# Gate products of a linear recurrence: one fp32 product, or three one-pass products of split operands, in a decoder layer on one Trainium2 core

## The chip, the cores and the metric

The kernel runs on one core of a Trainium2 chip, as one program. The metric is the device time of one execution in microseconds (us). Engines are named as in the profile: PE is TensorE (matrix products), PEld its weight loads, DVE VectorE, ACT ScalarE, POOL GpSimd, SP the queue that issues most transfers from memory.

## The reference, cut to what matters

One layer of a hybrid decoder is computed for 256 prompt tokens and 8 sample tokens (264 columns in all, `N`), with a model width of 2048, everything in float32. The first half of the layer is one combined projection of the normalised input, whose columns feed two groups: a gated linear recurrence (RG-LRU) and an mLSTM.

```
xn = rmsnorm(x);  z = xn @ w_in
xr, conv_new = causal_conv(z[rgx], conv_buf, conv_w, conv_b)      # 4 taps along the tokens
r  = sigmoid(block_diag(xr, w_rg_a, b_rg_a))                      # 8 blocks of 128 x 128
ig = sigmoid(block_diag(xr, w_rg_x, b_rg_x))
h  = rglru(xr, r, ig, lam, h0)                                    # scan over the tokens
y_rg = rmsnorm(h * gelu(z[rgg]))
h_ml = mlstm(q, k, v, logi, logf, C0, n0, m0)                     # q, k, v, gates also from z
y_ml = rmsnorm(h_ml, per head) * sigmoid(z[o])
x = x + concat(y_rg, y_ml) @ w_out
x = x + cross_attention(rmsnorm(x), memory);  x = x + swiglu(rmsnorm(x));  y = rmsnorm(x)
```

The two `block_diag` products are the gates of the title: for each of eight blocks of 128 channels, two products of a 128x128 weight with the block's 264 convolved tokens.

## The kernel before, in words

Tokens lie along the free axis, channels on the 128 partitions. All large products are built from one helper, `mm3`: both operands are split into a high part, rounded to the one-pass fp32r form, and a low part, the rest, and three one-pass products are added up (high by high, high by low, low by high). Weights arrive from memory by SP into `raw` tiles of 128x1024 and are split there: ACT copies the high half into a `W` tile (four buffers), DVE subtracts it from `raw` to make the low half. This is done per half step, one step ahead of PE (`LS`), and the loads run three steps ahead (`LD`).

The main loop goes over `steps`. A step of the projection is one tile of 128 output columns: 16 chunks by three products, 48 matmuls of 128x264 in a bank of PSUM (`mm`). Steps 0 to 7 give the convolution's inputs (rgx), step 8 the mLSTM's exponent gates, 9 to 16 q and k, 17 to 24 v, 25 to 32 rgg, 33 to 40 the output gate o, then w_out and the rest. The result of a step is evacuated by DVE and ACT one step later (`pend`); the evacuations of steps 4, 5 and 34 to 36 are held back, and the latter are run at the end of step 36:

```
if i not in (4, 5, 34, 35, 36):
    ... for e, x in pend: e(x)
ps = pef(i)
if i == 36:
    ... for e, x in pend: e(x)
```

All other work is written as generators ("side work") that are advanced after each step as far as the engines' clocks of a price table allow (`pump`; a `yield` gives the work back to the loop, `yield STEP` to the next step). Small products of PE that belong to side work are inserted into the steps' matmuls by `later(..., after=k)`: not before k more groups of three products have been issued. `finish(cond)` issues all such products that are outstanding at once. From this program order a scheduler builds the queue of each engine; the queues of SP are issued as written.

What the change and the prediction touch: `evac_rgx(n)` scales a block of rgx by `rstd` (the first norm) into a tile `z`; `rg_conv(n)` runs the four taps on DVE with a temporary `t` and leaves `xr`; `rg_gen` loads the gate weights (`wrg`, two transfers), runs the convolution and the two gate products of each block, and then the recurrence. The products stand in banks of tag `ax`. `ml_norm` is the norm at the end of the mLSTM: `sums` adds up squares on PE, from which DVE makes the small tiles `r`, `v`, `f` (128x12, `c` in the profile); `turn` transposes `f` by three products with the identity, ACT and DVE split the result into `hl` (4x264), and `scale(h)` spreads it over the partitions by two products a head:

```
later(lambda h=h: sums(h), after=1)
later(turn, after=19)
later(lambda h=h: scale(h), after=1 if h else 6)
```

`evac_o(0)`, the evacuation of the first o step, needs the normed heads: it calls `finish(lambda: ml.get("nn", 0) > j // 2)`. Tiles of tag `B` (128x1088) have 26 buffers, `t` six; every engine instruction is recorded under line 63, that of the wrapper which adds up prices, so that the profile is read by tile names.

Of the kernel before, what the change touches and what calls it, by code (L numbers as in the profile page):

```python
# [10 lines left out]
F32 = mybir.dt.float32  # L11
F32R = mybir.dt.float32r
I32 = mybir.dt.int32
AF = mybir.ActivationFunctionType
# [3 lines left out]
P = 128  # L18
# [4 lines left out]
N = T + NS  # L23
# [21 lines left out]
STEP = object()  # L45
# [45 lines left out]
def layer_kernel(ctx: ExitStack, tc, xT, memT, vec, wrg, w_in, w_out, w_q, w_k, w_v, w_o,  # L91
# [3 lines left out]
    act, dve, pe = Engine(nc.scalar, price_act), Engine(nc.vector, price_dve), Engine(nc.tensor, price_pe)  # L95
# [10 lines left out]
    def nm(s):  # L106
        uid[0] += 1
        return f"{s}_{uid[0]}"

    def view(t, shape, skip=0):  # L110
        v = t[:, skip: skip + int(np.prod(shape[1:]))]
        if len(shape) == 2:
            return v
        names = "abcd"[:len(shape) - 1]
        return v.rearrange(f"p ({' '.join(names)}) -> p {' '.join(names)}",
                           **{c: int(n) for c, n in zip(names[1:], shape[2:])})

    def B(shape, dt=F32, skip=0):
        return view(sb.tile([P, SLOT], dt, tag="B", bufs=NB, name=nm("B")), shape, skip)
# [109 lines left out]
    def mm3(ps, a, b, start, stop):  # L229
        ah, al = a  # L230
        bh, bl = b
        pe.matmul(ps, ah, bh, start=start, stop=False)
        pe.matmul(ps, ah, bl, start=False, stop=False)
        return pe.matmul(ps, al, bh, start=False, stop=stop)
# [65 lines left out]
    def bank(tag="mm"):  # L300
        return psm.tile([P, 512], F32, tag=tag, bufs=4, name=nm(tag))
# [26 lines left out]
    def V(name, j=0, w=1):  # L328
        o = _V[name][0] + j
        return vecs[:, o: o + w]  # L330
# [119 lines left out]
    rg = {"zn": 0}  # L450
# [39 lines left out]
    def evac_rgx(n):  # L490
        def f(ps):
            if "xr" not in rg:
                rg["xr"] = Arr(RGB)
            z = B([P, 2, 292])
            zi = z[:, 0, :]
            dve.memset(zi[:, 0:3], 0.0)
            smp = zi[:, 259:291].rearrange("p (b j) -> p b j", j=4)
            hist = V("cst", n * 24, 24).rearrange("p (b j) -> p b j", j=3)
            act.activation(smp[:, :, 0:3], hist, AF.Copy)
            dve.tensor_mul(zi[:, 3:259], ps[:, :T], rstd[:, :T])  # L500
            dve.tensor_mul(smp[:, :, 3:4], ps[:, T:N].rearrange("p (b j) -> p b j", j=1),
                           rstd[:, T:N].rearrange("p (b j) -> p b j", j=1))
            rg["z", n] = z
            if n >= 4:
                rg["zn"] = n + 1
        return f

    def rg_conv(n):
        z = rg.pop(("z", n))
        zi, t = z[:, 0, :], z[:, 1, :]  # L510
        smp = zi[:, 259:291].rearrange("p (b j) -> p b j", j=4)
        act.activation(cpo[:, n, :], zi[:, 256:259], AF.Copy)
        act.activation(cso[:, n, :, :], smp[:, :, 1:4], AF.Copy)
        w = [V("cw", j * 8 + n) for j in range(4)]
        dve.tensor_scalar(t[:, :288], zi[:, 0:288], w[0], V("cb", n), op0=OP.mult, op1=OP.add)
        dve.scalar_tensor_tensor(t[:, :288], zi[:, 1:289], w[1], t[:, :288], op0=OP.mult, op1=OP.add)
        dve.scalar_tensor_tensor(t[:, :288], zi[:, 2:290], w[2], t[:, :288], op0=OP.mult, op1=OP.add)
        xr = rg["xr"](n)
        dve.scalar_tensor_tensor(xr[:, :T], zi[:, 3:259], w[3], t[:, :T], op0=OP.mult, op1=OP.add)
        ts = t[:, 259:291].rearrange("p (b j) -> p b j", j=4)  # L520
        dve.scalar_tensor_tensor(xr[:, T:N].rearrange("p (b j) -> p b j", j=1), smp[:, :, 3:4], w[3],
                                 ts[:, :, 0:1], op0=OP.mult, op1=OP.add)

    def rg_gen():
        wr = [B([P, 8, P]), B([P, 8, P])]
        for j in range(2):
            sp.dma_start(wr[j], wrg[:, j * 8: j * 8 + 8, :])
        r, ig = Arr(RGB), Arr(RGB)
        for n in range(RGB):
            while rg["zn"] <= n:  # L530
                yield STEP
            rg_conv(n)
            yield STEP
            for t, j, b in ((r, 0, "ba"), (ig, 1, "bx")):
                ps = bank("ax")
                pe.matmul(ps[:, :N], wr[j][:, n, :], rg["xr"](n), start=True, stop=True)
                last = act.activation(t(n), ps[:, :N], AF.Sigmoid, bias=V(b, n))
            yield 0.1
        yield STEP
        xr, c = rg["xr"], rg["c"]  # L540
        e2 = Arr(RGB)

        for q in range(2):
            for n in range(4 * q, 4 * q + 4):
                with tc.issue_after(last.ins):
                    act.activation(e2(n), r(n), AF.Exp, scale=c[:, 8 + n: 9 + n])
                    le = act.activation(r(n), r(n), AF.Exp, scale=c[:, n: n + 1])
            dve.tensor_scalar(e2.tile(q), e2.tile(q), 1.0, -1.0, op0=OP.min, op1=OP.add)
            dve.tensor_mul(ig.tile(q), ig.tile(q), xr.tile(q))
            yield 2.0  # L550
        rg["le"] = le
        while "emc" not in ml:
            yield STEP
        for q in range(2):
            with tc.issue_after(ml["emc"].ins):
                act.activation(e2.tile(q), e2.tile(q), AF.Sqrt, scale=-1.0)
            dve.tensor_mul(ig.tile(q), ig.tile(q), e2.tile(q))
            yield 1.2
        h = Arr(RGB)
        rg["h"] = h  # L560
        for n in range(RGB):
            dve.tensor_tensor_scan(h(n)[:, :T], r(n)[:, :T], ig(n)[:, :T], 0.0, op0=OP.mult, op1=OP.add)
            yield 0.6
        h0 = V("h0", 0, 64).rearrange("p (n b) -> p n b", b=NS)
        for q in range(2):
            hq, rq_, iq = (t.tile(q)[:, :, T:N] for t in (h, r, ig))
            dve.tensor_mul(hq, rq_, h0[:, 4 * q: 4 * q + 4, :])
            dve.tensor_add(hq, hq, iq)
            act.activation(hlast[:, 4 * q: 4 * q + 4, :], h.tile(q)[:, :, T - 1: N], AF.Copy)
        pool_e.dma_start(o_h, hlast)  # L570
        pool_e.dma_start(o_cp, cpo)
        pool_e.dma_start(o_cs, cso)
        yield 0.3
# [882 lines left out]
    for i, (src, cols, pef, evf, need) in enumerate(steps):  # L1456
        load_piece(i + LD - 1)
        if i == 5:
            st["rg"] = side(rg_gen(), 0)
# [17 lines left out]
        ps = pef(i)  # L1477
# [141 lines left out]
```

## Time and the profile before

| | before |
|---|---|
| runs | 1540.1, 1539.87, 1538.17 us |
| median | 1539.87 us |
| the profiled execution: its own time | 1535.74 us |
| its span (first to last instruction) | 1534.0 us |
| mean granted clock of TensorE | 0.998 |
| busy: PE, DVE, ACT, POOL | 1524.8, 1059.3, 784.0, 126.1 us |
| share of the span: PE, DVE, ACT, POOL | 99%, 69%, 51%, 8% |
| PE's matmuls | 12028 |

The profile is of a single execution; its time is 4.1 us under the median of the runs. Busy times are sums over all instructions of an engine. Idle time before an instruction is put down to what released it. In the rows of groups a form such as `128*128 128x264` is the weight tile and the moving tile; "x48" is the number of instructions in a row. Positions in the text are microseconds from the start of the span.

### The profile page before, as it was taken

The page shows a single profiled execution, that of the slowest core. Times are in us where ns is not written, and L with a number is a line of the kernel's source. Part 1 is how long each engine was busy: PE and PEld are TensorE (multiplying, and loading weights), DVE is VectorE, ACT ScalarE, POOL GpSimd, SP SyncE. Part 2 cuts the span into 40 slices and gives each one's busy share as a digit, 9 for nine tenths or more (in the row PEclk, how much of TensorE's full clock was granted, in tenths as well). Part 3 has the DMA queues.
Part 4 walks back from the last instruction along what each step waited for, and adds up shares of the span by engine and source line. Part 5 has one row for each costly group of instructions (what it writes and reads, how often), then busy time and mean ns, then how long its engine had stood idle before and what let it go on. Part 6 is the DMA issues. An engine that isn't in the chain of part 4 may idle for free.

```text
span 1534.0 us, 29990 instructions
## 1 busy us (share of the span) xinstructions
PE 1524.8 (99%) x12028; PEld 1490.9 (97%) x12028; DVE 1059.3 (69%) x2013; ACT 784.0 (51%) x1234; POOL 126.1 (8%) x189
## 2 busy tenths in 40 slices
PE   9999999999999999999999999999999999999998
PEld 9999999999998888899999999999999999999997
DVE  7976988778898989966665555545555545555554
ACT  7555875655556666654444444334444433344463
POOL 0001210000223434400000000000000000000000
PEclk9999999999999999999999999999999999999999
DMA  8646996556798788755555555555555555555563
GB/s 300 203 154 203 322 327 207 194 179 233 266 341 326 246 339 332 248 160 188 188 180 182 190 179 184 188 179 184 188 179 185 187 180 186 185 180 186 158 225 121
DMA packets 94043, 329.17 MB, mean 215 GB/s; under 512 B 10992, under 2 KB 12448, under 8 KB 93904
## 3 DMA queue, kind: packets, MB, share of 16 engines
q1 hardware_dynamic: 78768, 274.62, 53.2%
q0 software_dynamic: 14992, 52.63, 9.7%
q8 instruction: 94, 1.54, 0.4%
q14 instruction: 45, 0.37, 0.1%
q10 hardware_dynamic: 144, 0.01, 0.0%
HBM read 314.36 MB, written 12.86 MB: 213 GB/s over the span
## 4 chain that ended last, share of the span: by engine, by line
PE 99%; DVE 0%; DMA 0%; ACT 0%; DVEq 0%; issue 0%; ACTq 0%
PE mm L63 94%; PE ax L63 5%; DVE B L63 0%; DMA raw<-w_in 0%; ACT W L63 0%; ACT B L63 0%; DVEq L1596 0%; ACTq L63 0%
## 5 line engine op out<-in xcount | busy, mean ns | idle before, releaser
L63 PE MATMUL mm<-B,W 128*128 128x264 f32 (+2 forms) x11008 | 1363.0, 285 | 0.0
L63 PEld LDWEIGHTS mm<-B,W 128*128 128x128 f32 x11008 | 1340.5, 188 | 11.7
L63 ACT ACTIVATE W<-raw 128x1024 fp32r<-128x1024 f32 (+2 forms) x520 | 536.7, 1034 | 640.3 <-PE mm L63 434.2
L63 DVE TENSOR_TENSOR W<-raw,W 128x1024 fp32r<-128x1024 f32 (+2 forms) x520 | 619.4, 1193 | 347.4 <-ACT W L63 346.0
L63 PE MATMUL mm<-W,B 128*128 128x512 f32 x384 | 92.4, 395 | 0.0
L63 PEld LDWEIGHTS mm<-W,B 128*128 128x128 f32 x384 | 70.9, 188 | 16.1
L63 DVE TENSOR_TENSOR t<-mm,rstd 128x264 f32<-128x264 f32 x104 | 44.7, 431 | 44.2 <-PE mm L63 44.1
L1511 POOL TENSOR_TENSOR B<-B,rstd 128x264 f32<-128x264 f32 x4 | 2.8, 738 | 854.1 <-ACT rstd L63 854.1
L63 DVE TENSOR_TENSOR xres<-xres,mm 128x264 f32<-128x264 f32 (+1 forms) x81 | 34.2, 423 | 37.8 <-PE mm L63 37.8
L63 DVE SCALAR_TENSOR_TENSOR B<-B,dw 128x256 f32<-128x256 f32 x128 | 53.8, 474 | 1.8 <-ACT dw L63 1.7
L63 DVE SCALAR_TENSOR_TENSOR dw<-B,qsm,dw 128x256 f32<-128x256 f32 x96 | 50.7, 537 | 2.3 <-ACT dw L63 1.9
L1142 POOL TENSOR_TENSOR dr<-dw,dr 128x256 fp32r<-128x256 f32 x32 | 38.4, 1200 | 102.7 <-ACT dr L63 102.6
L63 PE MATMUL ax<-B,B 128*128 128x256 f32 (+2 forms) x272 | 44.7, 303 | 0.0
L63 PEld LDWEIGHTS ax<-B,B 128*128 128x128 f32 x272 | 38.5, 190 | 2.4
L63 ACT ACTIVATE B<-xres,vecs 128x264 fp32r<-128x264 f32 (+1 forms) x64 | 31.0, 502 | 1.2 <-DMA xres<-xT 0.8
L1131 POOL DMA_DIRECT2D B<-kcT x32 | 17.4, 544 | 137.1 <-DVE B L63 127.2
L63 ACT ACTIVATE dw<-B,qsm 128x256 f32<-128x256 f32 x32 | 16.3, 508 | 22.4 <-DVE B L63 8.9
L63 ACT ACTIVATE B<-t 128x264 fp32r<-128x264 f32 (+1 forms) x60 | 24.5, 408 | 4.4 <-DVE t L63 4.4
L63 ACT ACTIVATE t<-xres 128x264 f32<-128x264 f32 (+2 forms) x46 | 18.7, 409 | 14.5 <-DVE xres L63 14.5
L63 ACT ACTIVATE t<-t 128x264 f32<-128x264 f32 (+1 forms) x61 | 24.7, 406 | 1.6 <-DVE t L63 1.5
L63 ACT ACTIVATE t<-B,B 128x128 f32<-128x128 f32 x64 | 20.1, 389 | 7.3 <-DMA B<-scr 7.3
L63 DVE SCALAR_TENSOR_TENSOR B<-xres,vecs,B 128x264 fp32r<-128x264 f32 x48 | 22.4, 486 | 0.6 <-ACT B L63 0.5
(166 smaller groups left out, 655.1 us busy)
## 6 DMA issues: line engine op xcount, KB each, us to landing
raw<-w_gu SPq DMA_DIRECT2D x176, 512.0 KB, 3.6
raw<-w_d SPq DMA_DIRECT2D x80, 512.0 KB, 3.6
raw<-w_in SPq DMA_DIRECT2D x78, 512.0 KB, 4.9
raw<-w_out SPq DMA_DIRECT2D x32, 512.0 KB, 3.7
raw<-w_q SPq DMA_DIRECT2D x32, 512.0 KB, 5.4
B<-kcT POOLq DMA_DIRECT2D x32, 512.0 KB, 8.3
B<-vcT POOLq DMA_DIRECT2D x32, 512.0 KB, 9.5
raw<-w_k SPq DMA_DIRECT2D x32, 512.0 KB, 6.5
```

The costliest lines, as they stand in the source:

```text
L63: return f(*a, **k)
L1131: pool_e.dma_start(kc, kcT[h, b])
L1142: pool_e.tensor_sub(wr[:, 1], acc, wr[:, 0].bitcast(F32))
L1511: e.tensor_mul(st["y"](c), st["y"](c), r)
```

## The change

The gate products become `mm3` products. The two weight tiles are split once into four tiles `gw` (high and low side by side, four blocks each), ACT copying the high part and DVE subtracting; the splits wait one step after the loads are issued. The convolved tokens of each block are split in the same way into `x2`, two blocks to a tile. Each gate is then three one-pass products instead of one fp32 product, which the hardware runs in several passes. To hold the number of `B` tiles, the convolution's inputs `z` share a tile by threes, and so do its temporaries `t`, which had lain beside `z`.

```diff
@@ evac_rgx
-            z = B([P, 2, 292])
-            zi = z[:, 0, :]
+            if ("zt", n // 3) not in rg:
+                rg["zt", n // 3] = B([P, 3, 292])
+            z = zi = rg["zt", n // 3][:, n % 3, :]
@@ rg_conv
-        z = rg.pop(("z", n))
-        zi, t = z[:, 0, :], z[:, 1, :]
+        zi = rg.pop(("z", n))
+        if n % 3 == 0:
+            rg["t"] = B([P, 3, 292])
+        t = rg["t"][:, n % 3, :]
@@ rg_gen
             sp.dma_start(wr[j], wrg[:, j * 8: j * 8 + 8, :])
+        yield STEP
+        gw = {}
+        for q in range(2):
+            for j in range(2):
+                gw[j, q] = B([P, 4, 2 * P], F32R, skip=48)
+                src = wr[j][:, 4 * q: 4 * q + 4, :]
+                act.activation(gw[j, q][:, :, 0:P], src, AF.Copy)
+                dve.tensor_sub(gw[j, q][:, :, P:], src, gw[j, q][:, :, 0:P].bitcast(F32))
+                yield 0.7
         r, ig = Arr(RGB), Arr(RGB)
         for n in range(RGB):
             while rg["zn"] <= n:
                 yield STEP
             rg_conv(n)
+            if n % 2 == 0:
+                x2 = B([P, 4, N], F32R)
+            xh, xl = x2[:, n % 2 * 2, :], x2[:, n % 2 * 2 + 1, :]
+            act.activation(xh, rg["xr"](n), AF.Copy)
+            dve.tensor_sub(xl, rg["xr"](n), xh.bitcast(F32))
             yield STEP
             for t, j, b in ((r, 0, "ba"), (ig, 1, "bx")):
                 ps = bank("ax")
-                pe.matmul(ps[:, :N], wr[j][:, n, :], rg["xr"](n), start=True, stop=True)
+                w = gw[j, n // 4][:, n % 4, :]
+                mm3(ps[:, :N], (w[:, 0:P], w[:, P:]), (xh, xl), True, True)
```

How the queues stand is shown at three places. The first is ACT after the first norm (about 40 us): `rstd` is the norm, `B_57` and `B_58` are the tiles with `wrg`, `B_59` and `B_60` inputs of the convolution, `W_65` (before) and `W_61` (after) the high half of step 7's first split, `B_73` to `B_76` the tiles `gw`. Before:

```order
L63 ACTIVATE rstd_96<-ax_42_444 128x264
L63 ACTIVATE cpo_97<-B_59_590 128x3
L63 ACTIVATE cso_98<-B_59_590 128x24
L63 ACTIVATE W_65_620<-raw_50_519 128x8x128
L63 ACTIVATE cpo_97<-B_60_595 128x3
L63 ACTIVATE cso_98<-B_60_595 128x24
```

After:

```order
L63 ACTIVATE rstd_96<-ax_42_444 128x264
L63 ACTIVATE B_73_704<-B_57_586 128x4x128
L63 ACTIVATE cpo_97<-B_59_590 128x3
L63 ACTIVATE cso_98<-B_59_590 128x24
L63 ACTIVATE W_61_616<-raw_50_519 128x8x128
L63 ACTIVATE cpo_97<-B_60_595 128x3
L63 ACTIVATE cso_98<-B_60_595 128x24
L63 ACTIVATE cpo_97<-B_59_590 128x3
L63 ACTIVATE B_74_707<-B_58_587 128x4x128
L63 ACTIVATE B_75_710<-B_57_586 128x4x128
L63 ACTIVATE B_76_713<-B_58_587 128x4x128
```

The first weight split of the gates now stands ahead of the split of step 7's weights in ACT's queue, the other three behind it.

The second place is PE at the end of step 36. `mm_378` (before) and `mm_382` (after) are its products; `ax_367` or `ax_378` from `ident` and `c` is `turn`, and the products with `ident_r` are `scale`. Before:

```order
L63 MATMUL ax_367_3110<-ident_70,c_366_3109 4x128 x2
L63 MATMUL ax_367_3110<-ident_70,c_366_3109 4x8
L63 MATMUL mm_378_3208<-B_20_183,W_370_3115 128x264
L63 MATMUL mm_378_3208<-B_21_184,W_370_3115 128x264
L63 MATMUL mm_378_3208<-B_20_183,W_370_3115 128x264 x2
L63 MATMUL mm_378_3208<-B_21_184,W_370_3115 128x264
L63 MATMUL mm_378_3208<-B_20_183,W_370_3115 128x264 x2
L63 MATMUL mm_378_3208<-B_21_184,W_370_3115 128x264
L63 MATMUL mm_378_3208<-B_20_183,W_370_3115 128x264 x2
L63 MATMUL mm_378_3208<-B_21_184,W_370_3115 128x264
L63 MATMUL mm_378_3208<-B_20_183,W_370_3115 128x264
L63 MATMUL ax_380_3265<-B_368_3111,ident_r_79 128x264
```

After:

```order
L63 MATMUL mm_382_3239<-B_20_183,W_370_3171 128x264 x2
L63 MATMUL mm_382_3239<-B_21_184,W_370_3171 128x264
L63 MATMUL mm_382_3239<-B_20_183,W_370_3171 128x264
L63 MATMUL ax_378_3231<-ident_70,c_377_3230 4x128 x2
L63 MATMUL ax_378_3231<-ident_70,c_377_3230 4x8
L63 MATMUL ax_386_3327<-B_379_3232,ident_r_79 128x264
L63 MATMUL ax_387_3332<-B_379_3232,ident_r_79 128x264
L63 MATMUL ax_388_3337<-B_379_3232,ident_r_79 128x264
L63 MATMUL ax_389_3342<-B_379_3232,ident_r_79 128x264
```

The transposition has moved behind the step's last product, next to the spreading products.

The third is DVE at the same place. `W_377` and `W_391` (before) and `W_398` (after) are low parts of weights, `W_391` (before) that of step 38's first half and `W_398` (after) that of its second; `c_366` and `c_377` are the factors `f`, `c_373` and `c_384` a temporary of its square root, `B_368` and `B_379` the split of the transposed factors, `lt` and `B_196` belong to the recurrence's output. Before:

```order
L63 TENSOR_TENSOR W_377_3205<-raw_362_3104,W_377_3205 128x8x128
L63 SCALAR_TENSOR_TENSOR c_373_3163<-c_373_3163,c_365_3108 128x12
L63 SCALAR_TENSOR_TENSOR c_366_3109<-c_373_3163,c_366_3109 128x12
L63 TENSOR_TENSOR c_373_3163<-c_366_3109 128x12
L63 SCALAR_TENSOR_TENSOR c_373_3163<-c_373_3163,c_365_3108 128x12
L63 SCALAR_TENSOR_TENSOR c_366_3109<-c_373_3163,c_366_3109 128x12
L63 TENSOR_TENSOR c_366_3109<-c_366_3109,c_364_3107 128x12
L63 TENSOR_TENSOR W_391_3312<-raw_374_3198,W_391_3312 128x8x128
L63 TENSOR_TENSOR B_368_3111<-ax_367_3110,B_368_3111 4x264
```

After:

```order
L63 TENSOR_TENSOR t_396_3368<-mm_382_3239,rstd_96 128x264
L63 SCALAR_TENSOR_TENSOR c_384_3284<-c_384_3284,c_376_3229 128x12
L63 SCALAR_TENSOR_TENSOR c_377_3230<-c_384_3284,c_377_3230 128x12
L63 TENSOR_TENSOR c_384_3284<-c_377_3230 128x12
L63 SCALAR_TENSOR_TENSOR c_384_3284<-c_384_3284,c_376_3229 128x12
L63 TENSOR_TENSOR W_398_3377<-raw_373_3225,W_398_3377 128x8x128
L63 TENSOR_TENSOR B_196_1827<-B_196_1827,lt_355_3063 128x264 x2
L63 SCALAR_TENSOR_TENSOR c_377_3230<-c_384_3284,c_377_3230 128x12
L63 TENSOR_TENSOR B_196_1827<-B_196_1827,lt_355_3063 128x264
L63 TENSOR_TENSOR c_377_3230<-c_377_3230,c_375_3228 128x12
L63 TENSOR_TENSOR B_379_3232<-ax_378_3231,B_379_3232 4x264
```

The last steps on `f`, which `turn` reads, stood ahead of both splits of step 38; they now stand behind the second, and behind the evacuation of step 36's products.

## The prediction

> **What bounds the kernel now.** I read the page's first part, then the chain that ended last, then the list of waits of TensorE (PE).
>
> ```profile
> PE 1524.8 (99%) x12028; PEld 1490.9 (97%) x12028; DVE 1059.3 (69%) x2013; ACT 784.0 (51%) x1234; POOL 126.1 (8%) x189
> ...
> PE mm L63 94%; PE ax L63 5%; DVE B L63 0%; DMA raw<-w_in 0%; ACT W L63 0%; ACT B L63 0%; DVEq L1596 0%; ACTq L63 0%
> ```
>
> ```profile
> PE mm L63 <- DVE ones L63: 1.1, 1, 1.1
> PE ax L63 <- ACT B L63: 0.4, 1, 0.4
> ```
>
> PE is busy for 99% of the span and 99% of the chain lies on it; it waits twice, 1.5 us in all, both times at the start. So what PE saves counts in full, what VectorE (DVE) or ScalarE (ACT) do more costs nothing by itself, and any place where PE has to wait counts in full too, since nothing later makes it up. The question is only whether PE gets work off, and whether the new order makes it wait. The average hides one thing: in the stage of the gates DVE is full.
>
> ```profile
> 40.00:60.00 20.00, 20.00 (x166) 19.86 (x166) 19.67 (x53) 10.29 (x26) 0.00 (x0) 1.00 0.63 210
> 60.00:80.00 20.00, 20.00 (x159) 19.61 (x158) 18.42 (x49) 11.08 (x19) 1.27 (x2) 1.00 0.61 191
> 80.00:100.00 20.00, 20.00 (x158) 19.61 (x158) 18.90 (x43) 10.28 (x13) 0.52 (x1) 1.00 0.49 160
> ```
>
> In each row of 20 us the fourth figure is DVE's busy time: 19.67, 18.42 and 18.90.
>
> **Part 1, the gate products.** The chain in order of time shows each pair of them (two fp32 products, four records) as a piece of its own between the steps' matmuls:
>
> ```profile
> 58.17 0.89 PE ax L63 x4
> ...
> 61.03 5.75 PE mm L63 x48
> 66.78 0.89 PE ax L63 x4
> ...
> 105.82 0.89 PE ax L63 x4
> ```
>
> There are eight such pieces of 0.89 us, the first and the last shown: 7.12 us. A one-pass matmul of the same 264 columns takes 5.75 / 48 = 0.120 us in the row between. The change makes six of a pair: 0.72 us, eight times 5.76 us. PE saves 1.36 us. Bounds: if the short groups of six ran no better than the pair does (0.148 us each), the saving is 0; more than 1.4 no row supports. I take 1.36, since the new products have the form of the steps' own.
>
> **Part 2, the added splits.** Four weight splits of 128x512 and eight token splits of 128x264 go to ACT and to DVE. The rows with the same sizes are 0.63 us (ACT) and 0.69 (DVE) for 512 columns, in the fence below, and 0.38 and 0.42 for 264 columns, in the next: some 5.5 us more on ACT, 6 us more on DVE. ACT is half idle there. DVE is not, so this moves its queue back; the cover is the lead of the W splits over PE. The tightest place is the first, where the weight splits wait for the wrg transfers:
>
> ```profile
> L527 SPq DMA_DIRECT2D B<-wrg x2: 424/425/426, 36.7 to 37.2; - x2
> ...
> DMA to landing us min/median/max: 7.7/8.0/8.4
> ```
>
> ```profile
> 39.73 18.44 PE L63 MATMUL mm<-B,W 128*128 128x264 f32 x152
> 41.09 1.06 ACT L63 ACTIVATE W<-raw 128x1024 fp32r<-128x1024 f32 x1
> 46.83 0.63 ACT L63 ACTIVATE W<-raw 128x512 fp32r<-128x512 f32 x1 [1.81 <-PE mm L63]
> 47.31 1.22 DVE L63 TENSOR_TENSOR W<-raw,W 128x1024 fp32r<-128x1024 f32 x1
> 50.59 0.69 DVE L63 TENSOR_TENSOR W<-raw,W 128x512 fp32r<-128x512 f32 x1
> ```
>
> The first half of wrg lands at 36.7 + 7.7 = 44.4, the second at 45.6. The first weight split now stands ahead of ACT's W split that ran at 41.09, so that one moves to 45.5, and DVE's first gate subtraction starts at 45.0. Up to the end of DVE's second W split of step 7 the new order has 7.6 us of work (two W of 1.14 from start to start, four subtractions of 0.6, three first convolution terms 1.0, three further terms 1.3, one evacuation 0.4, the rest small): ready at 52.6, against 48.5 before. PE wants that half at the 107th of the 152 matmuls, at 39.9 + 107 x 0.12 = 52.7. So this costs between 0 and, with a landing later by half a us, 0.5 us; I take 0.1. Afterwards the lead of the W splits grows again to 2 us and more by the same adding up. Memsets, the shared z and t tiles and the DMAs (same two for wrg, same place on the queue of SP) I cost at nothing: none is on PE, and the DVE time that they take is in the sum above. POOL's only move is one state load that now stands behind the hidden-state store.
>
> **Part 3, what moves with it.** The gate products come up to one step later, and the mLSTM part, which waits for their exponentials, comes exactly one step of 48 matmuls later. The end of that part does not: the flush of `evac_o(0)` stays at the end of step 36. The order shows what falls together: the transposition of the norm's factors (`turn`, identity against c) stood 12 matmuls ahead of the spreading products (`scale`); now both stand at the end of step 36, with nothing between. I went through all waits of PE in both orders, and counted the matmuls between a waiting product and the PE work that its releaser needs. In the matmuls up to the point where both orders are alike again (from step 43) the least is 12 before, at this place; in the change it is 0 here, and 28 at the next place. In the trace of before:
>
> ```profile
> 246.09 0.64 PE L63 MATMUL ax<-ident,c 128*4 128x128 f32 x6
> 246.65 1.73 PE L63 MATMUL mm<-B,W 128*128 128x264 f32 x12
> 248.32 1.22 PE L63 MATMUL ax<-B,ident_r 4*128 4x264 f32 x8
> ```
>
> ```profile
> 244.81 1.06 ACT L63 ACTIVATE W<-raw 128x1024 fp32r<-128x1024 f32 x1 [1.50 <-issue]
> 246.76 0.38 ACT L63 ACTIVATE B<-ax 4x264 fp32r<-4x264 f32 x1 [0.89 <-PE ax L63]
> 248.47 1.06 ACT L63 ACTIVATE W<-raw 128x1024 fp32r<-128x1024 f32 x1 [1.33 <-PE mm L63]
> ```
>
> ```profile
> 242.23 0.16 DVE L63 TENSOR_TENSOR c<-c 128x12 f32<-128x12 f32 x1
> 242.43 0.38 DVE L63 SCALAR_TENSOR_TENSOR c<-c,c 128x12 f32<-128x12 f32 x2
> 242.84 0.17 DVE L63 TENSOR_TENSOR c<-c 128x12 f32<-128x12 f32 x1
> 243.03 1.22 DVE L63 TENSOR_TENSOR W<-raw,W 128x1024 fp32r<-128x1024 f32 x1
> ...
> 245.19 0.17 DVE L63 TENSOR_TENSOR c<-c,c 128x12 f32<-128x12 f32 x1
> 245.90 1.23 DVE L63 TENSOR_TENSOR W<-raw,W 128x1024 fp32r<-128x1024 f32 x1 [0.54 <-ACT W L63]
> 247.17 0.42 DVE L63 TENSOR_TENSOR B<-ax,B 4x264 fp32r<-4x264 f32 x1
> 248.42 0.43 DVE L63 TENSOR_TENSOR t<-mm,rstd 128x264 f32<-128x264 f32 x1 [0.83 <-PE mm L63]
> ...
> 253.07 1.11 DVE L63 TENSOR_TENSOR B<-B,lt 128x264 f32<-128x264 f32 x3
> ```
>
> Before, c was ready at 245.36 and `turn` at 246.09 had nothing to wait for; ACT and DVE made its high and low part (246.76 to 247.59) under the 12 matmuls. Now let T be the end of step 36's last matmul (248.4 in this trace). PE then stands at `turn`, which needs c; and in DVE's queue the last two steps of c stand behind the W split of step 38's second half, whose buffer PE frees only at T. So nothing of this can start before T. Counted on DVE: an evacuation that waits for T behind five small steps on c, done at T + 0.7; four more small steps on c, 0.8 (242.23 to 243.03 has four): T + 1.5. The W split could start at T + 0.1 + 1.1 (ACT at 248.47, 0.09 after PE; DVE follows ACT by 1.09 at 245.90), so it starts at T + 1.5 and gives way at T + 2.65. Two products with lt (0.35 each), a step on c (0.2), a third product (0.35), the last step on c (0.17): T + 4.05. Then `turn` 0.6, ACT's copy 0.4 (246.73 to 247.14), and only then the spreading products, at T + 5.1; DVE's low part (0.42) is just in time for the fourth. They end at T + 6.25, where PE has 0.56 + 1.15 = 1.7 us of work: 4.5 us of waiting. Bounds: 4.2 when the small steps are done before the W split could start, 5.0 when each hand-over costs 0.1 more. What is late next is nothing: step 37's and step 38's first W halves are split already, and DVE needs until T + 14.3 to have the first half of step 39, which PE wants at T + 17.8.
>
> **Part 4, the clock.** A pause of four us has another price. The end and the start of the trace show it:
>
> ```profile
> 1526.00:1526.50 0.50, 0.38 (x2) 0.00 (x0) 0.50 (x3) 0.08 (x1) 0.50 (x1) 1.00 0.74 260
> ...
> 1528.50:1529.00 0.50, 0.00 (x0) 0.00 (x0) 0.44 (x2) 0.00 (x0) 0.25 (x1) 0.72 1.00 384
> 1529.00:1529.50 0.50, 0.00 (x0) 0.00 (x0) 0.00 (x0) 0.00 (x0) 0.00 (x0) 0.50 1.02 385
> ```
>
> ```profile
> 5.34 4.85 PE L63 MATMUL ax<-B,W 128*128 128x264 f32 x20 [0.44 <-ACT B L63]
> ...
> 10.76 2.84 PE L63 MATMUL mm<-B,W 128*128 128x264 f32 x22
> ```
>
> PE's last product ends at 1526.4; the granted clock (the column of 1.00) is 0.72 in the half us from 1528.5 and 0.50 after: it fell to half 2.3 us after PE stopped. And at the start the same 264 columns take 4.85 / 20 = 0.24 us, twice 0.129, until PE had worked without a break from 5.34 to about 9.8. So after a pause of 4.05 us, broken by 0.6 us of `turn`, I expect half speed for about 4.4 us of work: 2.2 us lost, and `turn` itself slower by 0.2. Bounds: 0 (the clock holds), and 4.3 if it takes all of the 8.7 us from PE's first product to 9.8. I take 2.4.
>
> The Trainium skill, TensorE: Matmul & The Clock Gate, section on the HAM clock gate, says that the clock halves after an idle window of about 3.4 us, the windows running free of the kernel. By that rule, taken as a wholly idle window, a pause of 4.05 us holds one in about (4.05 - 3.4) / 3.4 = 0.2 of the cases, an estimate from the page, and the sum would mostly be the one without the clock. The trace speaks for a stricter gate: it fell with PE idle for 2.3 us. No run here shows a pause in the middle.
>
> **The sum.** -1.36 (gates) + 0.1 (step 7) + 4.5 (the pause) + 2.4 (the clock) = +5.6 us. On the profiled execution (span 1534.0, its own time 1535.74) that is 1541.4. The runs' median is 1539.87, 4.1 above the profiled one; the differences carry over, so I predict 1545.5.
>
> **Rivals.**
> - The pause without the clock: half speed doesn't come, because the 0.6 us of `turn` breaks the idle stretch. Against it is the row of the fall after 2.3 us, for it that this row is from the end of the kernel alone. -1.36 + 0.1 + 4.5 = +3.2: 1543.1.
> - Not slower: c is done before PE gets to `turn`. The point that decides is a chain after T of under 1.3 us, less than the W split's copy on ACT (1.06) and subtraction (1.23) alone; so it would take a W split that is not held by PE at T, against the order. Then -1.3: 1538.6.
> - Slower still: the first place is no near miss. If wrg lands 1.5 us later than in this trace (another order of the transfers at 37 us), PE waits 1.5 us in step 7 too, and the sum is +7.1: 1547.0.
> - The change does not do what it says on PE: six short products cost what the pair did. Then +7.0 with the clock, inside the case before in time.
>
> **Chances.** The forecast 0.51, the pause alone 0.29, not slower 0.11, slower still 0.09 (the last rival is counted in the forecast). 0.2% is 3.1 us, about what a measurement of this kernel can tell from no change. Slower by more: nearly all of the forecast (0.48), half of the pause alone (0.14), all of the slowest (0.09): 0.71. Within: 0.03 + 0.15 + 0.08 of the case that is not slower, whose sum of -1.3 lies inside the bound: 0.26. Faster: the 0.03 that is left of that case, for gains that no row here gives a price. The range leaves out the case that is not slower: from 1541.1 (the pause alone with its lower bound of 4.2 us, 1542.8, less the 1.7 us by which the lowest run lies under the median) to 1548.3 (all upper bounds: -1.36 + 0.5 + 5.0 + 4.3 = +8.4). Above and below it lie about 2 in 10. The forecast's own range is 1544.3 to 1547.
>
> **What would show it.** In the profile after: PE's waits hold one entry of about 4 us from DVE c at 247 to 252 us, and about 0.5 from ACT B behind it; the granted clock is 0.5 for some us from there; the eight pairs read x6 with 0.72 us each; c's last step stands after a W split; no wait at 52 us. It is wrong if PE shows no wait there, if the pairs still take 0.89, or if a wait shows at W in 45 to 60 us.

## The result and the profile after

| | before | changed |
|---|---|---|
| runs | seven, 1535.59 to 1540.10 us | seven, 1541.68 to 1546.53 us |
| median | 1538.73 us | 1545.06 us |
| ratio | | 1.0048, 95% interval 1.0038 to 1.0058 |
| profiled execution, its span | 1534.0 us | 1544.8 us |

The change costs 6.3 us by the medians and 7.4 us by the ratio (5.8 to 8.9). The two profiles lie 10.8 us apart, since that of before is of a short execution and that of the changed kernel of a long one; so one profile a kernel is too few to price the small entries, and a second one of the changed kernel stands below. The page's row of engines and PE's list of waits, of the changed kernel:

```profile
PE 1527.9 (99%) x12044; PEld 1494.4 (97%) x12044; DVE 1064.5 (69%) x2025; ACT 790.9 (51%) x1248; POOL 126.9 (8%) x189
```

```profile
PE ax L63 <- DVE c L63: 3.7, 1, 3.7
PE ax L63 <- DVE B L63: 2.3, 3, 1.1
PE ax L63 <- ACT B L63: 1.2, 2, 0.7
PE mm L63 <- DVE ones L63: 1.1, 1, 1.1
PE mm L63 <- DVE W L63: 0.9, 1, 0.9
```

The columns are the waiting work, what released it, the sum of the waits, their number and the longest. Where PE stood still for 1.5 us before, it now stands still for 9.2. The shares on the page hide it: PE is at 99% both times. The gates themselves became cheaper, as the chain in order of time shows (start, duration, pieces):

```profile
60.07 0.24 PE ax L63 x2
60.44 0.48 PE ax L63 x4
66.55 0.74 PE ax L63 x6
...
98.24 0.74 PE ax L63 x6
```

A pair of gates takes 0.72 to 0.74 us instead of 0.89, also where it is split around one matmul of a step (0.24 + 0.48). The place of the loss is the end of step 36, in PE's timeline (start, duration, work, and in brackets the idle time ahead and its releaser):

```profile
248.05 3.14 PE L63 MATMUL mm<-B,W 128*128 128x264 f32 x24
254.93 0.63 PE L63 MATMUL ax<-ident,c 128*4 128x128 f32 x6 [3.74 <-DVE c L63]
256.03 1.92 PE L63 MATMUL ax<-B,ident_r 4*128 4x264 f32 x8 [0.47 <-ACT B L63]
```

Step 36 ends at 251.19 (T). The transposition waits 3.74 us for the factors, the spreading products 0.47 more for ACT's copy, and then take 1.92 us instead of 1.22. DVE's timeline shows why the factors are late:

```profile
251.58 0.37 DVE L63 SCALAR_TENSOR_TENSOR c<-c,c 128x12 f32<-128x12 f32 x2
251.98 0.17 DVE L63 TENSOR_TENSOR c<-c 128x12 f32<-128x12 f32 x1
252.19 0.17 DVE L63 SCALAR_TENSOR_TENSOR c<-c,c 128x12 f32<-128x12 f32 x1
252.36 1.23 DVE L63 TENSOR_TENSOR W<-raw,W 128x1024 fp32r<-128x1024 f32 x1
253.51 0.77 DVE L63 TENSOR_TENSOR B<-B,lt 128x264 f32<-128x264 f32 x2
254.19 0.17 DVE L63 SCALAR_TENSOR_TENSOR c<-c,c 128x12 f32<-128x12 f32 x1
254.27 0.43 DVE L63 TENSOR_TENSOR B<-B,lt 128x264 f32<-128x264 f32 x1
254.62 0.17 DVE L63 TENSOR_TENSOR c<-c,c 128x12 f32<-128x12 f32 x1
```

The last two steps on `c` stand behind the W split, for which ACT's half (251.28 to 252.34) could start only after T, and behind products with `lt` (two ahead of the first, a third ahead of the last). The last one ends at 254.79, T + 3.60, and PE goes on 0.14 us later. The windows (busy times of the engines, then the granted clock, the DMA share and GB/s) show the second price:

```profile
253.00:255.00 2.00, 0.07 (x1) 0.10 (x2) 1.78 (x6) 0.00 (x0) 0.00 (x0) 1.00 0.50 147
255.00:257.00 2.00, 1.53 (x11) 1.31 (x11) 0.42 (x1) 0.38 (x1) 0.00 (x0) 0.84 0.58 219
257.00:259.00 2.00, 2.00 (x10) 1.76 (x9) 1.67 (x5) 0.00 (x0) 0.00 (x0) 0.50 0.04 10
...
263.00:265.00 2.00, 2.00 (x18) 2.00 (x18) 1.72 (x5) 1.53 (x3) 0.00 (x0) 0.95 0.00 0
```

The clock is at half from 256.4 to 263.2. And smaller waits stand at three places where before had none: two at the sample part of the mLSTM, one at a weight tile, one at the sums of the recurrence's norm:

```profile
165.28 0.47 PE L63 MATMUL ax<-B,ident_r 4*128 4x256 f32 x2 [0.16 <-DVE B L63]
166.78 0.92 PE L63 MATMUL ax<-B,B 128*128 128x256 f32 x4 [1.03 <-DVE B L63]
...
220.91 14.41 PE L63 MATMUL mm<-B,W 128*128 128x264 f32 x118 [0.90 <-DVE W L63]
...
236.56 0.39 PE L63 MATMUL ax<-B,ones_r 128*128 128x264 f32 x1 [1.12 <-DVE B L63]
```

**A ledger of PE's time.** All kernels reach the same four products, so the starts of these can be compared: the first transposition (39.14 in before), the transposition of the exponents (123.88; one step of 5.75 us later in the changed kernel), the spreading products (248.32) and the next product with `ones_r` (330.07). Each entry is the profile of that kernel less that of before, in us.

- "Start" is what the first place is late.
- "Gates" is the stretch from the first place to the second, less a wait for W in it, and less 5.75 us where there is one step more (a later stretch then has one step less, and gets it back).
- "Small waits" and "pause" are idle times ahead of the rows.
- "Clock" is what the transposition, the spreading products and all up to the last place take longer (in `unpriced`: the transposition and the step of 48 matmuls at half clock behind 161.42).
- "Rest" is what is left, idle stretches below 0.15 us among it.

The kernels below the first two lines are those of the experiments; `flush37` and what follows are told there.

| | start | gates | small waits | pause | clock | rest | sum at the last place |
|---|---|---|---|---|---|---|---|
| changed | 0.5 | -1.0 | 3.2 | 4.2 | 3.2 | 0.8 | 10.9 |
| changed, second profile | 1.3 | -1.3 | 1.2 | 4.2 | 2.7 | 0.3 | 8.4 |
| pause_alone | 0 | 0 | 0.3 | 4.2 | 2.8 | 0.1 | 7.4 |
| flush37 | 0.4 | -1.0 | 2.2 | 0 | 0 | 0.6 | 2.2 |
| splits37 | 0.6 | 0.1 | 1.2 | 0 | 0 | 0.6 | 2.4 |
| tiles_only | 0 | 0 | 0 | 0 | 0 | 0 | 0 |
| unpriced | 0.3 | -1.3 | 1.4 | 0 | 1.6 | 0.5 | 2.5 |
| flush37_s | -0.2 | -1.3 | 1.2 | 0 | 0 | 0.5 | 0.2 |
| unpriced_s | 0.6 | -1.3 | 0 | 0 | 0 | 0.3 | -0.4 |

The start is late before the gates begin; it varies from profile to profile, between -0.2 and 1.3 us. Each line is one execution, and not always a typical one: that of `flush37` is third from the slowest of 12 (1537.84 us, median 1536.56), that of `unpriced` the slowest of 11 (1538.50, median 1535.73).

### The profile page after: what moved, and what is told of

It reads as the page before. It is cut to its first block, busy times and chain, and to the rows that moved or that the text cites. A ratio compares the mean times of both kernels' runs of the same rounds, so it can differ in the third digit from the quotient of the medians.

```text
span 1544.8 us, 30046 instructions
## 1 busy us (share of the span) xinstructions
PE 1527.9 (99%) x12044; PEld 1494.4 (97%) x12044; DVE 1064.5 (69%) x2025; ACT 790.9 (51%) x1248; POOL 126.9 (8%) x189
## 4 chain that ended last, share of the span: by engine, by line
PE 92%; DVE 2%; issue 2%; DMA 2%; ACT 1%; POOL 0%; DVEq 0%; SPq 0%; POOLq 0%; ACTq 0%
PE mm L63 88%; PE ax L63 4%; DMA B<-scr 1%; DVE B L63 1%; DVE t L63 1%; DMA B<-wrg 1%; DVE W L63 0%; ACT t L63 0%; DMA xres<-xT 0%; ACT B L63 0%; ACT W L63 0%; POOL B L871 0%; POOL B L867 0%; ACT L63 0%; DVE acc_rg L63 0%
## 5 line engine op out<-in xcount | busy, mean ns | idle before, releaser
L63 DVE TENSOR_TENSOR B<-B,B 128x264 fp32r<-128x264 f32 (+7 forms) x28 | 19.7, 711 | 6.5 <-ACT B L63 6.5
```

The costliest lines, as they stand in the source:

```text
L63: return f(*a, **k)
```

## The experiments

My theory (A): the whole loss is the pause at the end of step 36 with the clock behind it, and it comes from the order alone, the mLSTM one step later against a flush that stays. The rivals: the added work on DVE is what costs, wherever the flush is (B); the pause costs no clock (C).

**The changed kernel again** (`after_again`), for a second profile.

> The changed kernel once more, for a second profile. Its first profile is 10.8 us longer than that of before, while the medians differ by 6.3. Theory A: the pause at the end of step 36 is built into the order, so a wait of 3.6 to 3.9 us for c and one of 0.4 to 0.6 for B return, with half clock behind them (together about 8 us); the three smaller waits of the first profile (1.2 us at 165, 0.9 at 221, 1.1 at 236) hang on when transfers land and come and go, so they sum to anything from 0 to 3.2. Time: before + 5 to + 9 us. Rival B: the three smaller waits come from the added work on DVE and return with the same size (3.2 us together within 0.5), and then before + 8 to + 11.

Median 1543.55 us, ratio 1.0042 (1.0030 to 1.0054). PE's timeline:

```profile
252.94 1.05 PE L63 MATMUL ax<-ident,c 128*4 128x128 f32 x6 [3.74 <-DVE c L63]
254.46 2.12 PE L63 MATMUL ax<-B,ident_r 4*128 4x264 f32 x8 [0.47 <-ACT B L63]
```

Here the clock falls before PE goes on (0.81 in this row, in which PE does nothing), so the transposition runs at half clock too (1.05 us instead of 0.63):

```profile
252.50:252.75 0.25, 0.00 (x0) 0.00 (x0) 0.25 (x2) 0.00 (x0) 0.00 (x0) 0.81 0.83 246
```

The pause returns to the hundredth; the small waits return only in part (1.2 us instead of 3.2, none at 221), against rival B of this run. So the pause belongs to the order, and the small waits to the order and to the execution.

**The flush one step later** (`flush37`).

```diff
+        def early(ps):
+            z = zo[j] = tmp()
+            dve.tensor_mul(z, ps[:, :N], rstd)
+            act.activation(z, z, AF.Sigmoid)
         def f(ps):
-            z = tmp()
-            dve.tensor_mul(z, ps[:, :N], rstd)
-            act.activation(z, z, AF.Sigmoid)
+            if j not in zo:
+                early(ps)
+            z = zo[j]
...
+        if i in (34, 35, 36, 37):
+            with tc.high_priority(300):
+                pend[-1][0].early(pend[-1][1])
-        if i not in (4, 5, 34, 35, 36):
+        if i not in (4, 5, 34, 35, 36, 37):
...
-        if i == 36:
+        if i == 37:
```

> The changed kernel with the flush one step later: the o evacuations of steps 33 to 36 are parted, the first two operations (product with rstd, sigmoid) run in time and free the bank, the rest runs at the end of step 37. So the transposition stands 12 matmuls ahead of the spreading products again, as before the change, and PE has a whole step between the last sums and the flush. Theory A (the pause with its clock is the whole loss): no wait over 0.5 us at c, clock 1.00 through 240 to 275, and the time is before - 1.0 (gates) plus what the small waits leave, so ratio 0.999 to 1.001. Rival B (the loss sits in the work that DVE has more of, wherever the flush is): the wait turns up one step later with 2 us or more, and ratio 1.003 or more.

Median 1536.56 against 1536.30 us, ratio 0.9998 (0.9990 to 1.0007): the whole loss is gone, with gates and splits as in the changed kernel.

```profile
254.04 0.63 PE L63 MATMUL ax<-ident,c 128*4 128x128 f32 x6
254.61 1.72 PE L63 MATMUL mm<-B,W 128*128 128x264 f32 x12
256.26 1.22 PE L63 MATMUL ax<-B,ident_r 4*128 4x264 f32 x8
```

Twelve matmuls stand between the two again, no row has a wait, the spreading products take 1.22 us, the clock is 1.00. Rival B falls as the cause of the loss. What B is right about: in this profile 2.2 us of small waits stay (0.4 at 53, 1.2 at 165, 0.6 at 235), more than the gates save.

**The pause alone** (`pause_alone`), in the kernel before.

```diff
@@ ml_norm, after the sums of squares
         yield STEP
+        yield STEP
```

> The kernel before, gates untouched; only the norm of the mLSTM waits one step more before its sums (a second hand-back to the loop). Sums, transposition and spreading products stand at the same matmuls as in the changed kernel (1718 to 1736, 1760, 1760). Theory A: the order alone makes the pause: waits of 3.7 + 0.5 us and half clock for about 6.4 us (3.3 lost), so before + 7.5, ratio 1.0045 to 1.0055. Rival C (the pause without its clock): + 4.2, ratio 1.0027. Rival B (the added DVE work is needed): c is ready earlier, the wait is under 2 us and the clock stays, ratio under 1.0015.

Ratio 1.0043 (1.0030 to 1.0056), the same as the changed kernel's in the same session (1.0042), without a single changed gate.

```profile
251.83 0.82 PE L63 MATMUL ax<-ident,c 128*4 128x128 f32 x6 [3.74 <-DVE c L63]
253.12 2.12 PE L63 MATMUL ax<-B,ident_r 4*128 4x264 f32 x8 [0.47 <-ACT B L63]
```

The clock is at half behind it (0.50 in this row):

```profile
255.00:257.00 2.00, 2.00 (x10) 1.83 (x9) 2.00 (x7) 0.00 (x0) 0.00 (x0) 0.50 0.00 0
```

The ratio is slightly under the range that I gave (1.0045), and far above rival C's 1.0027 and B's 1.0015; the interval excludes both.

**The pause filled** (`warm`): 15 dummy products of PE stand in it, whose result nothing uses.

```diff
@@ turn
+            with tc.issue_after(st["mm"].ins):
+                for _ in range(15):
+                    pe.matmul(fp[:, 384:512], ones, ones, start=True, stop=True)
@@ where the products of a step are issued
+            st["mm"] = m
```

> The changed kernel with 15 dummy products (fp32, 128x128, result not used) between step 36's last product and the transposition, where PE stands idle. At the start of the trace eight such products took 3.78 us at half clock, so they fill about 3.5 us at full clock. Theory A: the wait stays as time, filled now, and the clock stays at 1.00, so the changed kernel - 3.3 us or more (before + 2 to + 4, ratio 1.0015 to 1.0025). Rival C (the half clock has another cause than PE's idle time, say the load of the chip at that place): the clock falls as in the changed kernel and the time is the same as that, ratio 1.004 to 1.006.

```profile
248.04 3.51 PE L63 MATMUL ax<-ones 128*128 128x128 f32 x30
251.85 0.64 PE L63 MATMUL ax<-ident,c 128*4 128x128 f32 x6 [0.30 <-DVE c L63]
252.96 1.32 PE L63 MATMUL ax<-B,ident_r 4*128 4x264 f32 x8 [0.47 <-ACT B L63]
```

```profile
254.00:256.00 2.00, 2.00 (x17) 1.86 (x16) 2.00 (x7) 0.00 (x0) 0.00 (x0) 1.00 0.02 6
```

In this profile the clock stays at 1.00, and the median is 2.9 us under that of the changed kernel (1540.64 against 1543.55; ratio to before 1.0029, 1.0018 to 1.0040). That is about the clock's entry of the ledger, a little less than the 3.3 expected, and the ratio lies above the 1.0015 to 1.0025 expected. So PE's idle time is what brings the clock down. That the filling keeps it up in every execution is not shown: five of the six slowest of its 12 runs (1540.88 to 1546.13 us) have a mean granted clock of 0.995 to 0.997, the other runs 0.998 or 0.999, and the profiled one is among the latter.

**Half the filling** (`warm7`): 7 of the dummy products.

> The changed kernel with 7 dummy products instead of 15 in the pause: they fill 7 x 0.236 = 1.65 us, and PE is then idle for about 2.1 us, works 0.63 on the transposition, and waits 0.47 more. It asks how short a pause halves the clock. After the kernel's end the clock fell 2.3 us after PE stopped. Theory A (what counts is the idle share of a stretch of about 3.4 us that runs free of the kernel, as the three falls of 6.8 us each suggest): the clock falls in some executions and not in others; the times spread over 3 us or more between the level of the 15 dummies (before + 4.3) and that of the changed kernel (before + 6.5). Rival D (the clock falls only behind a stretch without any work, 3.4 us long): it never falls, and all times are at the level of the 15 dummies, before + 3.5 to + 5.

```profile
251.64 0.64 PE L63 MATMUL ax<-ident,c 128*4 128x128 f32 x6 [2.09 <-DVE c L63]
```

```profile
254.00:255.00 1.00, 1.00 (x7) 1.00 (x7) 1.00 (x4) 0.00 (x0) 0.00 (x0) 0.80 0.02 8
255.00:256.00 1.00, 1.00 (x6) 1.00 (x6) 1.00 (x4) 0.00 (x0) 0.00 (x0) 0.50 0.00 0
...
258.00:259.00 1.00, 1.00 (x10) 1.00 (x9) 1.00 (x3) 1.00 (x4) 0.00 (x0) 0.99 0.00 0
```

The clock fell 1.9 us after the spreading products had begun, and for 3.4 us (254.6 to 258.0). Rival D is out: no stretch without work was longer than 2.1 us. The spread that A had expected did not show (five runs within 1.1 us; ratio 1.0033, 1.0021 to 1.0045), so whether the clock falls in only some of the executions stays open.

**Splits without the products** (`splits37`), on top of the later flush: the splits are made, but the gates are computed from the unsplit operands in one fp32 product each.

```diff
-                w = gw[j, n // 4][:, n % 4, :]
-                mm3(ps[:, :N], (w[:, 0:P], w[:, P:]), (xh, xl), True, True)
+                pe.matmul(ps[:, :N], wr[j][:, n, :], rg["xr"](n), start=True, stop=True)
```

> The kernel of the run with the later flush, but the gates again as one fp32 product each from the unsplit operands; the splits are still made and not read. It parts the products' saving from the cost of the splits. Theory A: eight pairs read 0.89 us instead of 0.73, so 1.2 to 1.3 us more than that run (which was 0.9998 of before), the same small waits at 53, 165 and 235 us (together 1 to 2.5 us): ratio to before 1.0004 to 1.0015. Rival: the three short products are themselves what PE waits around (banks, weight loads), then the small waits vanish with them and the time is that of before or below, 0.999 to 1.000.

Ratio 1.0008 (1.0000 to 1.0017), 0.0010 over that of `flush37` in another session, with intervals that overlap. The pairs in the chain:

```profile
59.92 0.89 PE ax L63 x4
...
112.26 0.89 PE ax L63 x4
```

In the ledger the gates' stretch is 1.1 to 1.4 us longer than in `flush37` and `flush37_s`, as expected. Of the small waits, those at 167 (0.5) and 235 (0.7) stay and the one at 53 does not come, so the rival, that the short products bring them, falls for the first two.

**The tiles alone** (`tiles_only`): the kernel before with `z` and `t` shared by threes.

> The kernel before with only the tiles of the convolution's inputs and temporaries shared by threes; gates and splits as before. I costed this part at nothing. Theory A: ratio 0.9993 to 1.0007, no wait of PE over 0.3 us after the start. Rival: blocks that share a tile wait for each other on DVE and the last pair of gates comes later, so the mLSTM loses cover: a wait of 0.5 to 1.5 us at 160 to 235, ratio 1.0004 to 1.001.

Ratio 1.0004 (0.9995 to 1.0013); its profile has no wait after the start, and all places of the ledger agree with before within 0.05 us.

**Splits outside the price table** (`unpriced`): the added four lines call the engines directly, so that the pacing of the side work does not count them.

```diff
-                act.activation(gw[j, q][:, :, 0:P], src, AF.Copy)
-                dve.tensor_sub(gw[j, q][:, :, P:], src, ...)
+                act._engine.activation(gw[j, q][:, :, 0:P], src, AF.Copy)
+                dve._engine.tensor_sub(gw[j, q][:, :, P:], src, ...)
...
```

> The changed kernel with the added splits left out of the table of prices that paces the side work; nothing else is changed, the splits run as before. The mLSTM's sums, transposition and spreading products then stand at the matmuls of the kernel before (1670 to 1688, 1748, 1760), one step earlier than in the changed kernel, with DVE carrying the same added work. Theory A (the pause comes from the one step of delay against the fixed flush): no pause over 0.5 us at 245 to 260, clock 1.00; time before - 1.0 plus small waits, ratio 0.9990 to 1.0005. Rival B (DVE is the bound in the gates' stage and needs the step): c is late again or PE waits for W at 55 to 75 us, 2 us or more in all, ratio 1.001 or more.

Ratio 0.9996 (0.9987 to 1.0005). The mLSTM stands in its old place, there is no pause, and DVE carries the added work: what delayed the mLSTM by a step was the price table's count of the added work, not the work. The wait is at another place:

```profile
161.42 0.66 PE L63 MATMUL ax<-ident,B 128*128 128x128 f32 x4 [1.41 <-DVE B L63]
```

```profile
162.00:164.00 2.00, 2.00 (x12) 2.00 (x11) 2.00 (x7) 2.00 (x5) 0.54 (x1) 0.55 0.95 209
164.00:166.00 2.00, 2.00 (x13) 2.00 (x12) 2.00 (x9) 2.00 (x5) 0.00 (x0) 0.60 0.97 371
```

In this execution an idle stretch of 1.41 us was enough for half clock over 3.4 us (162.2 to 165.6), which doubled its price. It is the slowest of the eleven and the one with the lowest mean clock (0.997, the others 0.998 or 0.999), so a wait and a fall of this size are not what the median shows.

**Where the small wait at 161 to 167 us comes from** (`flush37_s`, `unpriced_s`). The chain ahead of it begins with rows (`scr`) that are read back from memory by POOL's queue and spread over the partitions. In the ten profiles up to here the wait follows their landing (ACT's first work on them), counted from the last transposition of the exponents: 12.07 in before and 11.86 in `tiles_only`, no wait; 12.35 in `warm`, none; 12.39 in `warm7`, 0.2; 12.63, 0.5; 12.90, 0.7; 13.43 and 13.48, 1.2; 13.68 in `unpriced`, 1.4. (`pause_alone` is outside this row: 11.34, and 0.3 at the product ahead.) In the changed kernel the store of the hidden state stands ahead of the first state load on that queue, and the load goes out 7 us later, shortly ahead of the rows; in `unpriced` the load stands in its old place, but the store goes out 2 us ahead of the rows' reads. Both experiments put the store behind the mLSTM's last one.

```diff
@@ rg_gen
-        pool_e.dma_start(o_h, hlast)
@@ ml_sample, at its end
-                pool_e.dma_start(o_sc[h, :, b4 * 4: b4 * 4 + 4], C)
+                stored = pool_e.dma_start(o_sc[h, :, b4 * 4: b4 * 4 + 4], C)
+        with tc.issue_after(stored.ins):
+            pool_e.dma_start(o_h, hlast)
```

> The run with the later flush, and the store of the hidden state (o_h) issued behind the mLSTM's stores, so that on POOL's queue the first state load (c0T) no longer stands behind it and goes out some 7 us earlier, as in the kernel before. It asks where the small wait at 165 us comes from. Over the ten profiles so far the wait grows with the landing of the broadcast rows (scr): 0 up to 12.1 us after the last transposition of the exponents, 0.5 at 12.6, 0.7 at 12.9, 1.2 at 13.5. Theory E (the rows land late because the moved state load shares the transfers' time with them): landing at 12.2 or before, wait at 165 under 0.3 us, the wait at 235 unchanged at 0.5 to 1.1, and 0.8 to 1.2 us less than with the later flush alone: ratio 0.9988 to 0.9996. Rival F (the landing varies for another reason, the weights' loads): landing at 12.6 to 13.5 and the wait stays, ratio 0.9995 to 1.0005.

> The run without the splits in the price table, and the same move of the hidden state's store behind the mLSTM's stores. There the state load stood in its old place but the store came 3 us ahead of the reads of the rows, which landed at 13.7 (a wait of 1.4 us, and half clock for 3.4 us behind it). Theory E: landing at 12.2 or before, no wait over 0.3 us at 161, clock 1.00, ratio 0.9985 to 0.9993, which would be faster than the kernel before and than the changed one. Rival F: the wait stays with 0.5 us or more, ratio 0.9993 to 1.0003.

`flush37_s`: ratio 0.9993 (0.9984 to 1.0002), landing at 12.58, a wait of 0.38 at 165 and 0.79 at 233. `unpriced_s`: ratio 0.9995 (0.9986 to 1.0004), landing at 12.12, no wait at all. In its profile the rows (POOL's issue, ACT's first work):

```profile
144.90 1.11 POOL L870 DMA_DIRECT2D B<-scr  x2 [4.77 <-PE mm L63]
```

```profile
150.58 2.45 ACT L63 ACTIVATE t<-B,B 128x128 f32<-128x128 f32 x8 [4.95 <-DMA B<-scr]
```

They take 5.7 us here, 7.7 in `unpriced`, 5.15 in before. The direction is that of theory E, but neither run decides. `flush37_s` keeps a wait of 0.38 us (1.24 in `flush37`, 0.69 in the changed kernel's second profile), and its landing lies above E's 12.2. `unpriced_s` has E's landing and no wait, but its ratio lies in F's range, and is that of `unpriced` (0.9996) again. The landing in the changed kernel's own order ranged from 12.35 to 13.48; whether the moved store or the execution decides is open. `unpriced_s` and `flush37_s` lie some 0.5% under the changed kernel by these ratios; neither is clear of the kernel before.

## Why the prediction was right

**The sum.** +5.6 us was forecast, 1545.5; measured were 1545.06 and +6.3 us. The two largest terms were right in kind and place; the agreement to half a us is partly luck. The sum starts from the median of three runs of before (1539.87), while the four later values of it lie lower (1538.73, and 1536.1 to 1536.8 in the sessions of the experiments). And against the profile of before, on which the sum was made, the two profiles of the changed kernel are 8.3 and 10.8 us longer, not 5.6: small waits that the sum lacks, and a clock that it has too cheap, against a pause that it has too dear.

- **The gates**: -1.36 forecast, -1.0 to -1.3 measured. The pairs take 0.73 us rather than 0.72.
- **Step 7**: +0.1 forecast for a W half ready at 52.6. In the changed kernel:

```profile
45.13 0.63 ACT L63 ACTIVATE B<-B 128x512 fp32r<-128x512 f32 x1 [4.31 <-DMA B<-wrg]
...
52.07 1.22 DVE L63 TENSOR_TENSOR W<-raw,W 128x1024 fp32r<-128x1024 f32 x1
```

  The first weight split waits for `wrg` (45.13; 44.4 was laid out for its landing), and the half is ready at 53.29, just when PE wants it: no wait above 0.15 us is listed. With a landing some 0.2 us later, in `flush37`, PE waited 0.39, and in `warm`, where PE itself was earlier, 0.26: the bound of 0.5 held, but a wait for W at this place was named as a sign of being wrong, so the 0.1 is a matter of the execution.
- **The pause**: 4.5 forecast, 4.2 measured in three profiles (3.74 + 0.47). The chain on DVE was as laid out, with T + 3.6 for the last step on `c` instead of T + 4.05; the small steps were done when ACT released the W split at 252.36, which was the lower bound's condition (4.2).
- **The clock**: 2.4 forecast, 2.7 to 3.2 measured. It did fall, against the rival of the pause alone, in all three profiles with the full pause. The length was wrong: half speed lasted 6.8 us each time, 3.4 in `warm7` and `unpriced`, and not 4.4. The estimate from the rule of the Trainium skill, one fall in five, did not come: it was three in three.
- **What was not in the sum**: small waits of 1.2 to 3.2 us at 165, 221 and 235, and a rest of 0.3 to 0.8 us in the kernels with the splits (0 to 0.1 in the two without them). The step that failed is the search for other tight places. It counted, for each wait of PE, the matmuls since the PE work that the releaser needs, and found 28 or more. That count misses two things. A chain that begins with a transfer from memory, as the one at 165 does, has no such count: before, the rows land at 150.95, and what PE needs at 160.52 is ready at 160.02. (The prediction also put the move of a state load behind the hidden state's store at nothing; whether it costs anything is open.) And the count leaves out how full DVE is. The wait at 235 stands in all seven profiles in which the whole mLSTM comes one step later (0.54 to 1.12 us) and in none of the other five, so it belongs to the order, and only its size to the execution. PE waits there for the low half of the sum `acc_rg`, which DVE makes at 230.01 in before and at 236.08 in the changed kernel:

```profile
230.01 0.42 DVE L63 TENSOR_TENSOR B<-acc_rg,B 128x264 fp32r<-128x264 f32 x1
...
234.60 1.23 DVE L63 TENSOR_TENSOR W<-raw,W 128x1024 fp32r<-128x1024 f32 x1 [0.15 <-ACT W L63]
...
236.08 0.42 DVE L63 TENSOR_TENSOR B<-acc_rg,B 128x264 fp32r<-128x264 f32 x1
```

  Before, it is ready some 2.5 us ahead of PE, and DVE is busy for 5.3 of the 7 us from 225 to 232. In the changed kernel DVE still has work of the mLSTM's sample part there (7.0 of 7 us), and the subtraction comes behind a W split and an evacuation.
- **"What is late next is nothing"** held at the pause: behind it all profiles run alike.

The change does not lose because split products are slow, but because the pacing of the side work delays the mLSTM by a step, and the flush at the end of step 36 does not move with it. With the flush moved (`flush37`) or the delay taken away (`unpriced`), the change is worth nothing that can be measured. In the profiles its 1.3 us go into small waits elsewhere; `unpriced_s`, which has none, is 0.4 us shorter than before at the ledger's last place.

## What to carry to other kernels

When work is delayed against a point in the program that stays (here the flush), look at that point first: list what stands between the last two dependent products there, and which long job each small step on the other engines has got behind. A stop of the tensor engine can cost more than its own length: here 4.2 us of pause brought 2.7 to 3.2 us of slower clock. Where it cannot be avoided, cheap products can keep the clock up, as in the profile of `warm`. And a search for tight places must start chains at transfers too, with the spread of their landing, and ask how full the other engines are there, not only count from the engine that waits.

## What the runs showed of the hardware

- The clock fell with idle stretches of 3.74 + 0.47 us (three profiles of three), and also with shorter ones: 2.09 + 0.47 (`warm7`) and 1.41 us (`unpriced`), each in the one execution that was profiled. It held with 0.16 + 1.03 and with 1.12 in the changed kernel, and with 0.30 + 0.47 in `warm`. The fall trails PE's stop: by 5.2 us in the changed kernel, 3.4 in its second profile, 2.2 in `unpriced`. So it can come when PE is at work again; in the second profile it came 0.3 us before.
- Half speed then lasted 6.8 us (three falls) or 3.4 us (two), nothing between. The Trainium skill, TensorE: Matmul & The Clock Gate, in its part on the HAM clock gate, has free-running windows of about 3.4 us, and the lengths, one or two of them, agree with that. Its condition of an idle window does not: the stretch of 3.4 us up to the fall at 162.2 in `unpriced` held 2.0 us of work.
- The broadcast of the same rows took from 3.7 us (`pause_alone`) to 7.7 us (`unpriced`) from issue to use, with weights streaming beside it. In before it took 5.15 us, and what PE needs behind it was ready 0.5 us early.
